# The ends of a SwiGLU FFN in a one-core decoder trunk: later operand sums and transposes, a spilled residual moved in the program, and one 16-k-tile block in place of a reduced one

## The chip, the core and the metric

The kernel runs on one core of a Trainium2 chip. The metric is the device time of one execution in microseconds (us); what is given below is the median of three runs, beside one profiled execution that the trace was taken from. TensorE (PE) multiplies, VectorE (DVE) and ScalarE (ACT) work on tiles, GpSimd (POOL) and SyncE (SP) issue DMAs, each in the order of its own instruction stream.

## What is computed

A trunk of two layers over 256 positions of width 2048, all in float32. Layer 0 mixes with SSD heads and latent attention, layer 1 with stick-breaking attention; each layer ends in a SwiGLU FFN with a hidden width of 5632, and this is what the change is about:

```
for layer in range(2):
    h = rms_norm(x, mix_norm[layer])
    x = x + mixer(h)
    x = x + swiglu_ffn(rms_norm(x, ffn_norm[layer]), w_gate[layer], w_up[layer], w_down[layer])
return rms_norm(x, final_norm)

def swiglu_ffn(h, w_gate, w_up, w_down):
    return (silu(h @ w_gate) * (h @ w_up)) @ w_down
```

## The kernel before

**Products.** A float32 operand is kept as two parts, hi and lo (hi is the value cast to a shorter float, lo the rest), and a product is three matmuls: hi by weight-hi, lo by weight-hi, hi by weight-lo. Weights come from memory as tiles of 128 x 2048 (1 MB), four k-tiles of 128 rows by 512 columns; ACT casts the hi part into one of the tiles named wh (L316, through wsplit), DVE subtracts to leave lo in place (L322). Both are in program order on their engines, and PE reads them after. The row of a tile that PE needs next is therefore always "cast on ACT, then split on DVE".

**Blocks.** An FFN has eleven blocks of 512 hidden columns. `gate_up(n)` calls `pair`, which computes both gate and up for a block over all 16 k-tiles by a Strassen-like scheme: seven products M1 to M7 over the first eight k-tiles, on sums of operand tiles and of weight tiles (wsub, L673: tiles named wsum), and the plain products c0 to c3 over the other eight. This order is `HALF`. The order `MORE` runs the scheme over 12 k-tiles: in place of c0 and c1 stand four half-size tiles n0 to n3, whose weight sums are t1 to t4. HALF has 180 matmuls of 512 columns a block (7 x 12 + 4 x 24), MORE 174 (84 + 2 x 24 + 42). MORE needs the operand sums N, made by `more_sums` on DVE and ACT from the third quarter of the normed input (xT[2]). Before the change blocks n = 0 and 1 are HALF, blocks 2 to 10 MORE.

**Order of the work.** PE runs in program order. A generator task sleeps a number of steps, and a step is a call of `tick`: two in a product of four k-tiles, one a k-tile in `project`, so about six matmuls. `more_sums` sleeps 1 step after it is spawned and `transpose_split` for h (the block's output, which becomes the operand of the down projection) 6. The other engines are ordered by a scheduler from priorities: weights by a counter, transposes of h and evacuations as urgent.

**h and the residual.** `right` ends a block's hidden tile with L852 on DVE and sends it through a DMA on POOL's queue to a tile of another type ("s<-s", L855); PE transposes what has landed (L327). The residual sits in the tile xres. It is written to memory as four quarters (saved) as each is ready, by POOL DMAs in norm_block (L465) and norm_operand (L536); from block 1 on, `lend` gives xres's space to the weight pools as two slots (tiles named lent0 and lent1), and each down projection adds its part into saved by an accumulating DMA (L871). After block 10, `load_residual` reads saved back into xres (L552), and the last three blocks' down projection (12 k-tiles, four `project` calls, L421 to L424) adds to xres. Blocks 0 and 1 have no down projection behind them; after each block from 2 on run two `project` calls of 8 k-tiles.

Of the kernel before, what the change touches and what calls it, by code (L numbers as in the profile page):

```python
# [15 lines left out]
P = 128  # L16
# [5 lines left out]
HID = 5632  # L22
# [18 lines left out]
class Trunk:  # L41
# [289 lines left out]
    def transpose_split(self, src, res, g=None, wait=3, rank=None):  # L331

        for k2 in range(2):
            yield wait if k2 == 0 else 1
            pt = self.tr([2, S])
            for k in range(2):
                for t in range(2):
                    self.transpose(pt[:, k, t * P:(t + 1) * P], src(t, 2 * k2 + k))
            hi, lo = self.s2([2, S], F32R), self.s2([2, S], F32R)
            if g is None:  # L340
                with self.urgent() if rank == self.URGENT else self.priority(rank or self.tc.cur_priority):
                    self.split(hi, lo, pt)
            else:
                with self.urgent() if rank == self.URGENT else self.priority(rank or self.tc.cur_priority):
                    gk = [g[:, kk:kk + 1] for kk in (2 * k2, 2 * k2 + 1)]
                    for k in range(2):
                        act = self.nc.scalar.activation(hi[:, k], pt[:, k], AF.Copy, scale=gk[k])
                    for k in range(2):
                        dve = self.nc.vector.scalar_tensor_tensor(lo[:, k], pt[:, k], gk[k], hi[:, k].bitcast(F32),
                                                                  op0=ALU.mult, op1=ALU.subtract)  # L350
                if rank and rank >= 99000 and k2 == 0:
                    self.first = [act.ins, dve.ins]
            res.append((hi, lo))
# [101 lines left out]
    def norm_block(self, st, j, g, wait=2, rank=None, blocks=False, spill=None, pause=2):  # L455

        x, res = self.xres, []

        def gen():
            yield from self.transpose_split(  # L460
                lambda t, k: x[:, t, j * 512 + k * P:j * 512 + (k + 1) * P], res, g[:, 4 * j:4 * j + 4], wait, rank)
            for t in range(2):
                self.square_sum(x[:, t, j * 512:(j + 1) * 512], st["ssq"][:, t, j:j + 1])
            if spill is not None:
                self.nc.gpsimd.dma_start(spill[j], x[:, :, j * 512:(j + 1) * 512])  # L465
        st["xT"].append((self.spawn(gen()), res))
        if blocks and j == 1:
            self.make_sums(st, pause)
# [36 lines left out]
    def more_sums(self, st):  # L505

        sub = lambda o, p, q: self.nc.vector.tensor_tensor(o, p, q, op=ALU.subtract)
        add = lambda o, p, q: self.nc.vector.tensor_tensor(o, p, q, op=ALU.add)
        yield 1
        self.join(st["xT"][2][0])  # L510
        a = {}
        for j, (hi, lo) in enumerate(st["xT"][2][1]):
            r = self.s2([2, S])
            add(r, hi.bitcast(F32), lo.bitcast(F32))
            a.update({(t, j): r[:, :, t * P:(t + 1) * P] for t in range(2)})
        yield 1
        s12, s34 = self.s2([4, P]), self.s2([4, P])
        s1, s2, s3, s4 = s12[:, :2], s12[:, 2:], s34[:, :2], s34[:, 2:]
        add(s1, a[1, 0], a[1, 1])
        sub(s2, s1, a[0, 0])  # L520
        sub(s3, a[0, 0], a[1, 0])
        sub(s4, a[0, 1], s2)
        for s in (s12, s34):
            yield 1
            hi, lo = self.s2([4, P], F32R), self.s2([4, P], F32R)
            self.split(hi, lo, s)
            st["N"].append((hi, lo))

    def norm_operand(self, st, j, g):

        x = self.xres

        def squares():
            for t in range(2):
                self.square_sum(x[:, t, j * 512:(j + 1) * 512], st["ssq"][:, t, j:j + 1])
            self.nc.gpsimd.dma_start(self.saved[j], x[:, :, j * 512:(j + 1) * 512])  # L536
        self.operand_block(st, j, lambda t, k: x[:, t, j * 512 + k * P:j * 512 + (k + 1) * P],
                           g[:, 4 * j:4 * j + 4], squares, 9)

# [125 lines left out]
        w.left = uses  # L665
        return wh, wl, w

    def wsub(self, o, p, q, so=None, sp=None, sq=None):

        half = lambda w, n: w.raw if n is None else w.raw[:, 2 * n:2 * n + 2]  # L670
        with self.priority(self.wprio):
            self.wprio += 100
            ins = self.nc.vector.tensor_tensor(half(o, so), half(p, sp), half(q, sq), op=ALU.subtract).ins  # L673
        for w in (p, q):
            w.readers.append(ins)
        if not o.readers:
            self.filled(o, ins)
# [8 lines left out]

    LATE = ("M1", "M5", "M3", "M6", "M2", "M7", "M4", "c0", "c1", "c2", "c3")

    def pair(self, st, va, vb, left, right, order=HALF):

# [85 lines left out]
        for m in order:  # L778
            if m == "t1":
                src["n2"] = self.wsum()  # L780
                self.wsub(src["n2"], raw["c1"], raw["c0"], 0, 0, 0)
                continue
            if m == "t2":
                self.wsub(src["n2"], raw["c1"], src["n2"], 1, 1, 0)
                continue
            if m == "t3":
                self.wsub(raw["c1"], raw["c1"], raw["c1"], 0, 1, 0)
                continue
            if m == "t4":
                src["n3"] = self.wsum()  # L790
                self.wsub(src["n3"], raw["c0"], src["n2"], 0, 1, 1)
                continue
            if m == "n0":
                halves(self.wsplit(raw["c0"], 4, 4, mybir.DependencyClass.Sync), ("M1", True), ("M2", False))
                continue
            if m == "n2":
                halves(self.wsplit(src["n2"], 4, 4, mybir.DependencyClass.Sync), ("M5", True), ("M6", False))
                continue
            if m == "n1":
                halves(self.wsplit(raw["c1"], 4), ("M7", False), ("M3", False))  # L800
                continue
            if m == "n3":
                halves(self.wsplit(src["n3"], 2, 2), ("M4", False))
                continue
            if m == "M1":
                self.wsub(t1, b12, b11)
                if more:
                    load("c0", "c1")
            if m == "M5":
                self.wsub(t2, b22, t1)  # L810
            if m == "M3":
                self.wsub(b12, b22, b12)
            if m == "M6":
                load("b21")
                b21 = src["M2"] = raw["b21"]
                src["M4"] = self.wsum()
                self.wsub(src["M4"], b21, t2)
            if m[0] == "c":
                load(m)
                src[m] = raw[m]  # L820
            w = self.wsplit(src[m], 8 if m[0] == "c" else 4)
            if m[0] == "c":
                k0 = 8 + int(m[1]) // 2 * 4
                x = [[self.operand_tile(st, k0 + k, t) for k in range(4)] for t in range(2)]
                for b in ("z", "p3") if int(m[1]) % 2 else ("p2", "p4"):
                    add(b, x[b in ("z", "p4")], w)
                continue
            add(bank[m], ops(m), w, m if m in keeps else None)

    def lend(self):  # L830

# [4 lines left out]
    def ffn(self, layer, st, gain_next):  # L836
# [3 lines left out]
        h = [None, None]  # L840
# [16 lines left out]

        def gate_up(n):
            self.pair(st, self.cols(wg, n * 512), self.cols(wu, n * 512), left, right,
                      self.MORE if n >= 2 else self.HALF)  # L860
            res = []
            return self.spawn(self.transpose_split(
                lambda t, k, h=tuple(h): h[t][:, k * P:(k + 1) * P], res, wait=6, rank=self.URGENT)), res

        def down(act, n0, n):
            ps = self.project(self.pairs(act), self.cols(wd, n * 512, r0=n0 * 512), 4 * len(act))
# [4 lines left out]
                nc.gpsimd.dma_start(self.saved[n][:, t], s, accum_op=ALU.add)  # L871

        act, held = [], []
        for n in range(HID // 512):
            if n == 1:
                self.lend()
            act.append(gate_up(n))
            for c in held[:2]:
                down(*c)
            held = held[2:]  # L880
            if len(act) == 2 and n < 8:
                held = [(act, n - 1, c) for c in range(4)]
                act = []
        nst = self.norm_begin()
        self.slots["w"] = self.slots["w"][:self.LOW]
        self.slots["wsum"] = self.slots["wsum"][:self.SUMS]
        self.load_residual(lambda j: self.saved[j])
        for n in range(4):
            if gain_next is None:
                self.final(n, self.pairs(act), self.cols(wd, n * 512, r0=8 * 512), 12)  # L890
# [77 lines left out]
    def norm_next(self, st, n, g):  # L968
        if n < 2:
            self.norm_operand(st, n, g)  # L970
        else:
            self.norm_block(st, n, g, 2 if n == 2 else 6, self.URGENT, spill=self.saved)
            if n == 2:
                st["more"] = self.spawn(self.more_sums(st))

# [520 lines left out]
```

## Time and profile before

| | |
|---|---|
| median of three runs | 2420.68 us (2420.16 to 2421.95) |
| the profiled execution | 2423.95 us, its span 2422.2 us |
| mean granted TensorE clock | 0.996 |
| PE, DVE, ACT, POOL busy, share of the span | 98%, 83%, 60%, 10% |
| FFN of layer 0, first block's first product to last block's last | about 632 us to 1265 us into the span |
| FFN of layer 1, the same | about 1711 us to 2345 us |

The profile's rows name line, engine, operation and tile (out<-in, buffer numbers left out), the count, and the idle time of the engine ahead of them with what ended it. A row of the timeline begins with the start in us from the span's start and the length. PE's matmuls overlap in the rows (a 128x512 matmul lasts some 0.39 us in a row and the next one starts 0.23 us after it), so distances are read from start to start.

### The profile page before, as it was taken

The numbers are of one execution on the slowest core, as the hardware profiler recorded it, in microseconds if no ns is written. First come the engines' busy times: TensorE is split into PE (matmuls) and PEld (weight loads), VectorE is DVE, ScalarE is ACT, GpSimd is POOL, SyncE is SP. The second block draws the span as 40 slices with busy tenths as digits, with TensorE's granted clock in tenths as the row PEclk, the third lists the DMA queues.
The fourth block names the chain that finished last, engine by engine and source line by source line (L and its number), as shares of the span: only waits on it lengthen the run. The fifth ranks groups of instructions, "written<-read, shape, count | busy, mean of one in ns | idle before, by whom it ended". The sixth has DMA issues, their size and how long they took to land.

```text
span 2422.2 us, 28061 instructions
## 1 busy us (share of the span) xinstructions
PE 2382.6 (98%) x10936; PEld 1956.7 (81%) x10936; DVE 2007.2 (83%) x1664; ACT 1463.6 (60%) x1480; POOL 233.8 (10%) x301
## 2 busy tenths in 40 slices
PE   8999999999999999999999999999999999999998
PEld 7888888777778888888888888888778888888877
DVE  6776597578999888888887989779998888998874
ACT  6665465555755665656655686775655565666663
POOL 1342001120000000000010010000000000000011
PEclk9999999999999999999999999999999999999999
DMA  7655556434656777777776555556667777777773
GB/s 261 201 182 192 186 191 186 117 131 156 222 196 226 221 232 230 220 233 235 224 222 225 199 175 180 184 174 226 211 206 229 224 226 224 227 226 229 226 251 119
DMA packets 274902, 497.88 MB, mean 206 GB/s; under 512 B 22924, under 2 KB 48144, under 8 KB 274768
## 3 DMA queue, kind: packets, MB, share of 16 engines
q1 hardware_dynamic: 255440, 446.48, 55.7%
q0 software_dynamic: 18752, 48.55, 8.0%
q8 instruction: 86, 1.41, 0.2%
q10 hardware_dynamic: 576, 1.05, 0.1%
q14 instruction: 48, 0.39, 0.0%
HBM read 459.24 MB, written 25.20 MB: 200 GB/s over the span
## 4 chain that ended last, share of the span: by engine, by line
PE 73%; issue 13%; DVE 9%; DMA 2%; POOL 2%; ACT 1%; SPq 0%; POOLq 0%; DVEq 0%; ACTq 0%
PE acc L726 39%; PE acc L421 10%; PE acc L424 10%; PE acc L423 10%; DVE wsum L673 2%; DVE wsum L322 2%; DVE w L322 2%; DMA s<-s 1%; DVE lent L322 1%; DVE lent L673 1%; PE at L1341 1%; PE tr L327 1%; DVE w L673 0%; POOL s L1245 0%; DVE s L322 0%
## 5 line engine op out<-in xcount | busy, mean ns | idle before, releaser
L322 DVE TENSOR_TENSOR w<-w,wh 128x2048 fp32r<-128x2048 f32 (+2 forms) x397 | 885.8, 2242 | 199.4 <-ACT wh L316 189.4
L726 PE MATMUL acc<-wh,s 128*128 128x512 f32 x3888 | 991.6, 393 | 7.3 <-DVE s L322 3.1
L316 ACT CAST wh<-w 128x2048 fp32r<-128x2048 f32 (+2 forms) x397 | 741.6, 1874 | 350.1 <-PE acc L424 133.8
L726 PEld LDWEIGHTS acc<-wh,s 128*128 128x128 f32 x3888 | 727.4, 189 | 160.1 <-ACT s L747 4.3
L421 PE MATMUL acc<-wh,s 128*128 128x512 f32 (+1 forms) x1280 | 510.8, 399 | 2.0 <-ACT wh L316 2.0
L424 PE MATMUL acc<-wh,s 128*128 128x512 f32 (+1 forms) x1280 | 496.9, 388 | 0.0
L423 PE MATMUL acc<-w,s 128*128 128x512 f32 (+1 forms) x1200 | 464.9, 387 | 0.0
L726 PE MATMUL acc<-w,s 128*128 128x512 f32 x1304 | 355.7, 391 | 0.4 <-DVE w L322 0.4
L726 PEld LDWEIGHTS acc<-w,s 128*128 128x128 f32 x1304 | 245.7, 189 | 53.5 <-DVE w L322 1.8
L424 PEld LDWEIGHTS acc<-wh,s 128*128 128x128 f32 x1280 | 240.8, 188 | 50.3
L421 PEld LDWEIGHTS acc<-wh,s 128*128 128x128 f32 x1280 | 241.2, 188 | 48.0 <-ACT wh L316 2.4
L423 PEld LDWEIGHTS acc<-w,s 128*128 128x128 f32 x1200 | 226.3, 189 | 43.6 <-issue 1.4
L316 ACT CAST wh<-wsum 128x2048 fp32r<-128x2048 f32 x103 | 186.7, 1813 | 74.7 <-DVE wsum L673 53.3
L322 DVE TENSOR_TENSOR wsum<-wsum,wh 128x2048 fp32r<-128x2048 f32 x103 | 222.8, 2163 | 4.0 <-ACT wh L316 4.0
L316 ACT CAST wh<-lent 128x2048 fp32r<-128x2048 f32 (+1 forms) x66 | 120.5, 1836 | 75.4 <-DMA lent<-in_w_gate_dram 33.6
L322 DVE TENSOR_TENSOR lent<-lent,wh 128x2048 fp32r<-128x2048 f32 (+1 forms) x66 | 144.0, 2186 | 8.6 <-ACT wh L316 8.2
L673 DVE TENSOR_TENSOR wsum<-w,wsum 128x2048 f32<-128x2048 f32 (+1 forms) x52 | 106.1, 2041 | 25.0 <-PE acc L726 20.9
L726 PE MATMUL acc<-wsum,s 128*128 128x512 f32 x388 | 109.2, 396 | 5.9 <-DVE wsum L322 5.3
L747 ACT COPY s<-acc 128x512 f32<-128x512 f32 x132 | 77.0, 584 | 57.2 <-PE acc L726 57.0
L855 POOL DMA_DIRECT2D s<-s x44 | 24.5, 557 | 783.7 <-DVE s L852 733.9
L726 PEld LDWEIGHTS acc<-wsum,s 128*128 128x128 f32 x388 | 72.1, 189 | 26.3 <-DVE wsum L322 11.8
L871 POOL DMA_DIRECT2D saved<-s x64 | 56.5, 1026 | 331.1 <-ACT s L870 331.1
(262 smaller groups left out, 1868.6 us busy)
## 6 DMA issues: line engine op xcount, KB each, us to landing
w<-in_w_down_dram SPq DMA_DIRECT2D x78, 1024.0 KB, 5.0
w<-in_w_gate_dram SPq DMA_DIRECT2D x76, 1024.0 KB, 5.1
w<-in_w_up_dram SPq DMA_DIRECT2D x76, 1024.0 KB, 5.2
w<-in_w_qkv_dram SPq DMA_DIRECT2D x48, 1024.0 KB, 5.0
w<-in_w_in_dram SPq DMA_DIRECT2D x47, 1024.0 KB, 5.1
w<-in_w_out_even_dram SPq DMA_DIRECT2D x32, 1024.0 KB, 5.0
saved<-s POOLq DMA_DIRECT2D x64, 256.0 KB, 6.7
w<-in_w_out_odd_dram SPq DMA_DIRECT2D x16, 1024.0 KB, 4.9
```

What stands on the lines that cost most here:

```text
L316: cast = nc.scalar.copy(hi, src).ins
L322: return nc.vector.tensor_tensor(lo, src, hi.bitcast(F32), op=ALU.subtract).ins
L327: self.nc.tensor.transpose(out.bitcast(F32R), src, self.ident_r)
L421: nc.tensor.matmul(ps[t], hi[:, ts], wh, start=k == 0, stop=False)
L423: slot.used(nc.tensor.matmul(ps[t], hi[:, ts], wl, start=False, stop=False), self.clock)
L424: nc.tensor.matmul(ps[t], lo[:, ts], wh, start=False, stop=k == nk - 1)
L673: ins = self.nc.vector.tensor_tensor(half(o, so), half(p, sp), half(q, sq), op=ALU.subtract).ins
L726: m = nc.tensor.matmul(ps[b], x, y, start=b not in started, stop=stop, skip_group_check=True)
L747: self.kept = nc.scalar.copy(o, ps[b]).ins
L855: nc.gpsimd.dma_start(words.bitcast(F32), h[t])
L871: nc.gpsimd.dma_start(self.saved[n][:, t], s, accum_op=ALU.add)
L1341: nc.tensor.matmul(py[:, ds], rows[c, h // 4][:, h % 4], xdt[c][:, ds], start=True, stop=True)
```

## The change

Five edits. `more_sums` sleeps 40 steps instead of 1. The transposes of h sleep 10 steps instead of 6, but for the last block's, which stay at 6. MORE begins at block 3 instead of block 2. The writing of the residual is taken out of the norm blocks and made a task of the FFN (`residual_away`, four DMAs 4 steps apart, joined ahead of `lend`); reading it back is a task too (`residual_back`, 12 steps, then 6 each). And block 0's subtraction for M3 is told to stand behind the last operand split of the third quarter (`lo`) in the order of DVE.

```
     def more_sums(self, st):
...
-        yield 1
+        yield 40
         self.join(st["xT"][2][0])
...
     def norm_operand(self, st, j, g):
...
-            self.nc.gpsimd.dma_start(self.saved[j], x[:, :, j * 512:(j + 1) * 512])
...
-    def wsub(self, o, p, q, so=None, sp=None, sq=None):
+    def wsub(self, o, p, q, so=None, sp=None, sq=None, after=None):
...
-        with self.priority(self.wprio):
+        with self.priority(self.wprio), self.tc.issue_after(after) if after else nullcontext():
...
             if m == "M3":
-                self.wsub(b12, b22, b12)
+                self.wsub(b12, b22, b12, after=st["lo"] if after == "lo" else after)
...
+    def residual_back(self):
+        for j in range(4):
+            yield 12 if j == 0 else 6
+            self.nc.gpsimd.dma_start(self.xres[:, :, j * 512:(j + 1) * 512], self.saved[j])
+
+    def residual_away(self):
+        for j in range(4):
+            yield 4
+            self.nc.gpsimd.dma_start(self.saved[j], self.xres[:, :, j * 512:(j + 1) * 512])
...
-                      self.MORE if n >= 2 else self.HALF)
+                      self.MORE if n >= 3 else self.HALF, None if n else "lo")
...
-                lambda t, k, h=tuple(h): h[t][:, k * P:(k + 1) * P], res, wait=6, rank=self.URGENT)), res
+                lambda t, k, h=tuple(h): h[t][:, k * P:(k + 1) * P], res, wait=10 if n < HID // 512 - 1 else 6, rank=self.URGENT)), res
...
+        away = self.spawn(self.residual_away())
         for n in range(HID // 512):
             if n == 1:
+                self.join(away)
                 self.lend()
...
-        self.load_residual(lambda j: self.saved[j])
+        self.spawn(self.residual_back())
...
-            self.norm_block(st, n, g, 2 if n == 2 else 6, self.URGENT, spill=self.saved)
+            self.norm_block(st, n, g, 2 if n == 2 else 6, self.URGENT)
```

How this moves instructions, at three places. **VectorE, block 0 of layer 0's FFN, ahead of M6's split.** In the rows, w_77, w_79 and wsum_83 are the splits of c0, M3 and M6 (written as the low part), wsum_82 and w_76 are weight sums, s are operand tiles; the rows with s alone are the operand sums N and their splits. Before:

```order
L508 TENSOR_TENSOR s_650_4940<-s_643_4918,s_644_4919 128x512
L508 TENSOR_TENSOR s_651_4942<-s_646_4929,s_647_4930 128x512
L322 TENSOR_TENSOR w_77<-w_78,wh_67 128x2048
L508 TENSOR_TENSOR s_652_4952<-s_650_4940,s_651_4942 128x256
L507 TENSOR_TENSOR s_653_4953<-s_650_4940 128x256
L507 TENSOR_TENSOR s_652_4952<-s_652_4952,s_650_4940 128x256
L673 TENSOR_TENSOR w_76<-w_80,w_76 128x2048
L507 TENSOR_TENSOR s_653_4953<-s_651_4942,s_652_4952 128x256
L322 TENSOR_TENSOR s_656_4968<-s_652_4952,s_655_4967 128x512
L322 TENSOR_TENSOR w_79<-w_80,wh_68 128x2048
L322 TENSOR_TENSOR s_658_4980<-s_653_4953,s_657_4979 128x512
L673 TENSOR_TENSOR wsum_82<-w_70,wsum_84 128x2048
```

After (the lines are numbered two or so higher):

```order
L322 TENSOR_TENSOR w_77<-w_78,wh_67 128x2048
L560 TENSOR_TENSOR xres<-s_622_4732,xres 128x512
L349 SCALAR_TENSOR_TENSOR s_644_4925<-tr_4919,va,s_643_4924 128x256 x2
L349 SCALAR_TENSOR_TENSOR s_648_4945<-tr_4939,va,s_647_4944 128x256 x2
L675 TENSOR_TENSOR w_76<-w_80,w_76 128x2048
L322 TENSOR_TENSOR w_79<-w_80,wh_68 128x2048
L349 SCALAR_TENSOR_TENSOR s_654_4986<-tr_4980,va,s_653_4985 128x256 x2
L675 TENSOR_TENSOR wsum_82<-w_70,wsum_84 128x2048
L349 SCALAR_TENSOR_TENSOR s_657_5001<-tr_4995,va,s_656_5000 128x256 x2
L322 TENSOR_TENSOR wsum_83<-wsum_84,wh_65 128x2048
```

The eight sums and splits have left this place, and both pairs of L349 of the last quarter now stand ahead of wsum_83, where before the second pair stood behind it. The eight rows are found again in block 1, between M3's split and M4's.

**TensorE, the end of block 10 in layer 0.** L726 (L728 after) is a product of pair; acc is its sum, lent_91 and lent_93 are low parts in xres's space. Before, the pair's last rows are

```order
L726 MATMUL acc_8555<-wh_67,s_664_5020 128x512
L726 MATMUL acc_8555<-wh_67,s_665_5021 128x512
L726 MATMUL acc_8555<-wh_67,s_664_5020 128x512
L726 MATMUL acc_8555<-wh_67,s_665_5021 128x512
L726 MATMUL acc_8555<-lent_93,s_661_5005 128x512 x2
L726 MATMUL acc_8555<-lent_93,s_664_5020 128x512 x2
```

and the last products with a lent tile after the change are

```order
L728 MATMUL acc_8552<-wh_67,s_631_4794 128x512
L728 MATMUL acc_8552<-wh_67,s_632_4795 128x512
L728 MATMUL acc_8552<-lent_91,s_631_4794 128x512 x4
L728 MATMUL acc_8554<-wh_68,s_625_4760 128x512
L728 MATMUL acc_8554<-wh_68,s_626_4761 128x512
```

Which slot a tile gets has shifted, since block 2 makes fewer sums: the pair's last products no longer read a lent tile, and 78 matmuls of the pair follow those that do. The same holds in layer 1.

**GpSimd, the DMAs around block 10's h in layer 0.** s_898 and s_899 are the two halves of h. Before:

```order
L871 DMA saved_89<-s_888_8545 128x512
L871 DMA saved_89<-s_889_8548 128x512
L552 DMA xres<-saved_86 128x2x512
L552 DMA xres<-saved_87 128x2x512
L552 DMA xres<-saved_88 128x2x512
L855 DMA s_898_8773<-s_897_8744 128x512
L855 DMA s_899_8789<-s_894_8628 128x512
L552 DMA xres<-saved_89 128x2x512
```

After:

```order
L883 DMA saved_89<-s_888_8543 128x512
L883 DMA saved_89<-s_889_8546 128x512
L835 DMA xres<-saved_86 128x2x512
L835 DMA xres<-saved_88 128x2x512
L835 DMA xres<-saved_87 128x2x512
L835 DMA xres<-saved_89 128x2x512
L867 DMA s_898_8771<-s_897_8742 128x512
L867 DMA s_899_8787<-s_894_8626 128x512
```

All four reads of the residual now stand ahead of both halves of h. The four writes of the residual stand in POOL's order where they stood.

More of the change, by code (lines that the diff above doesn't have):

```diff
@@ L350, in transpose_split @@
                                                                   op0=ALU.mult, op1=ALU.subtract)
+                self.lo = dve.ins
                 if rank and rank >= 99000 and k2 == 0:
@@ L461, in gen @@
                 lambda t, k: x[:, t, j * 512 + k * P:j * 512 + (k + 1) * P], res, g[:, 4 * j:4 * j + 4], wait, rank)
+            if j == 2:
+                st["lo"] = self.lo
             for t in range(2):
@@ L687, with pair @@
     LATE = ("M1", "M5", "M3", "M6", "M2", "M7", "M4", "c0", "c1", "c2", "c3")
-    def pair(self, st, va, vb, left, right, order=HALF):
+    def pair(self, st, va, vb, left, right, order=HALF, after=None):
         nc = self.nc
```

## The prediction

> **What bounds the kernel now.** I began with the busy shares and then took the table of what PE waited for.
>
> ```profile
> PE 2382.6 (98%) x10936; PEld 1956.7 (81%) x10936; DVE 2007.2 (83%) x1664; ACT 1463.6 (60%) x1480; POOL 233.8 (10%) x301
> PE tr L327 <- DMA s<-s: 8.5, 6, 2.0
> PE acc L726 <- DVE wsum L322: 5.3, 2, 2.6
> ```
>
> PE is busy 98% of the span, so it is the bound, and only its waits and its number of matmuls can move the time. The columns of the waits are the sum in us, how often, and the longest. The two largest in the FFNs are the transposes of h, which wait for the DMA that changes h's type, and M6's product, which waits for its split. They are what the five edits touch, so I went to those places in the timeline. First block 0 of layer 0:
>
> ```profile
> 647.77 1.97 PE L726 MATMUL acc<-wh,s 128*128 128x512 f32 x8
> 652.38 1.20 PE L726 MATMUL acc<-wsum,s 128*128 128x512 f32 x4 [2.63 <-DVE wsum L322]
> 653.41 3.51 PE L726 MATMUL acc<-wh,s 128*128 128x512 f32 x8
> ```
> ```profile
> 686.79 1.07 PE L726 MATMUL acc<-w,s 128*128 128x512 f32 x4
> 689.59 0.51 PE L327 MATMUL tr<-ident_r,s 128*128 128x128 f32 x4 [1.73 <-DMA s<-s]
> ...
> 731.86 1.07 PE L726 MATMUL acc<-lent,s 128*128 128x512 f32 x4
> 733.49 0.51 PE L327 MATMUL tr<-ident_r,s 128*128 128x128 f32 x4 [0.56 <-DMA s<-s]
> ...
> 1273.14 0.39 PE L424 MATMUL acc<-wh,s 128*128 128x512 f32 x1
> 1275.18 0.50 PE L327 MATMUL tr<-ident_r,s 128*128 128x128 f32 x4 [1.66 <-DMA s<-s]
> ```
>
> Eight matmuls last 1.97 us and a single one 0.39, so one starts (1.97 - 0.39) / 7 = 0.2265 us after another. From start to start, less what the matmuls between need: M6 lost 652.38 - 647.77 - 8 x 0.2265 = 2.80 us; the transposes behind block 0 lost 1.89, those behind block 1 0.72, those behind block 10 1.81. Each is about 0.16 more than the idle time in brackets.
>
> Layer 1 has the same four places. Its waits from block 0 to the transposes behind block 1, and the row behind its block 10:
>
> ```profile
> PE tr L327 <- DMA s<-s: 2.9, 2, 2.0
> PE acc L726 <- DVE wsum L322: 2.6, 1, 2.6
> PE acc L726 <- DVE w L322: 0.2, 1, 0.2
> 2355.28 0.50 PE L327 MATMUL tr<-ident_r,s 128*128 128x128 f32 x4 [1.68 <-DMA s<-s]
> ```
>
> With 0.16 more for each, that is 2.80 for M6, 3.2 for the two pairs of transposes, 1.84 at the end. Together the two layers lose 5.6 at M6, 2.61 + 3.2 = 5.8 at the transposes behind blocks 0 and 1, and 3.65 behind block 10: **15.0 us**, and 0.2 at c0 in layer 1.
>
> Each wait can cost twice. The eight matmuls after M6's wait last 3.51 us instead of 1.97. Busy times in 3.4 us behind three of the waits (the figure ahead of DMA share and GB/s is the granted clock):
>
> ```profile
> 653.50:656.90 3.40, 3.40 (x10) 2.65 (x9) 3.40 (x3) 3.15 (x6) 0.00 (x0) 0.50 0.38 67
> 1275.00:1278.40 3.40, 3.22 (x19) 2.76 (x20) 1.13 (x3) 1.17 (x2) 0.00 (x0) 1.00 0.92 357
> 1769.70:1773.10 3.40, 3.40 (x14) 2.71 (x13) 0.83 (x2) 1.17 (x2) 0.00 (x0) 0.50 0.02 5
> ```
>
> Behind M6 and behind block 0's transposes, in both layers, the clock is 0.50 for 3.4 us (the first and the last of four such stretches are shown); behind block 10 it stays 1.00. Half speed over 3.4 us is 1.7 us lost: 4 x 1.7 = **6.8 us** hang on waits of 1.73 to 2.63 us. That the gate goes with the wait is what I take from it.
>
> [...]
>
> **Part a: operand sums 40 steps later.** DVE in block 0, from ahead of c0's split to M6's:
>
> ```profile
> 636.70 1.28 DVE L508 TENSOR_TENSOR s<-s,s 128x512 f32<-128x512 f32 x2
> 637.90 2.28 DVE L322 TENSOR_TENSOR w<-w,wh 128x2048 fp32r<-128x2048 f32 x1
> 640.10 0.42 DVE L508 TENSOR_TENSOR s<-s,s 128x256 f32<-128x256 f32 x1
> ...
> 641.11 2.28 DVE L673 TENSOR_TENSOR w<-w,w 128x2048 f32<-128x2048 f32 x1
> 643.31 0.41 DVE L507 TENSOR_TENSOR s<-s,s 128x256 f32<-128x256 f32 x1
> ...
> 644.25 2.28 DVE L322 TENSOR_TENSOR w<-w,wh 128x2048 fp32r<-128x2048 f32 x1
> 646.45 0.68 DVE L322 TENSOR_TENSOR s<-s,s 128x512 fp32r<-128x512 f32 x1
> 647.05 2.28 DVE L673 TENSOR_TENSOR wsum<-w,wsum 128x2048 f32<-128x2048 f32 x1
> 649.25 0.87 DVE L349 SCALAR_TENSOR_TENSOR s<-tr,va,s 128x256 fp32r<-128x256 f32 x2
> 650.04 2.28 DVE L322 TENSOR_TENSOR wsum<-wsum,wh 128x2048 fp32r<-128x2048 f32 x1
> ```
>
> DVE has no gap here. The sums and their splits take 637.90 - 636.70 = 1.20, 641.11 - 640.10 = 1.01, 644.25 - 643.31 = 0.94 and 647.05 - 646.45 = 0.60: 3.75 us that leave. By the order, the second pair of L349 comes ahead of M6's split (0.79, as the first pair: 650.04 - 649.25). So the split comes 2.97 us earlier, and PE, which read its result at 652.38, could at 649.41. PE itself is there at 647.77 + 8 x 0.2265 = 649.58: the wait goes, with 0.17 us to spare. That is thin, but a miss of 0.3 costs 0.3 and hardly the clock, which stayed at 1.00 behind 1.66 us. Telling block 0's subtraction for M3 to stand behind `lo` changes only this order and is in the count. Value: -2.80 a layer and -1.7 for the clock.
>
> The eight instructions come back in block 1, between M3's split and M4's. There DVE has room:
>
> ```profile
> 668.93 0.69 DVE L846 TENSOR_TENSOR s<-acc,s 128x512 f32<-128x512 f32 x1 [1.67 <-PE acc L726]
> 681.88 1.40 DVE L852 SCALAR_TENSOR_TENSOR s<-s,rstd,s 128x512 f32<-128x512 f32 x2
> ...
> 697.15 2.29 DVE L322 TENSOR_TENSOR lent<-lent,wh 128x2048 fp32r<-128x2048 f32 x1
> 704.66 1.07 PE L726 MATMUL acc<-lent,s 128*128 128x512 f32 x4
> ```
>
> M4's split (the lent tile) was done at 699.4, and PE came to it at 704.66, 5.2 us later. After the change PE comes 8.1 us earlier (2.80 + 1.7 + 1.89 + 1.7), at 696.6. DVE starts the stretch behind L852 5.4 us earlier (next part) and must do 3.75 us more in it and one weight sum of 2.2 us that the order shows moved behind L852; it saves the gaps in which it stood waiting for h's transposes, and those now come later. Adding the rows of the order from 677.8 on, each by its length here, gives M4's split ready at about 696.1 and M7's at 698.9 against 699.3: estimates with half a microsecond to spare. I take nothing for it; the upper bound is a rival.
>
> **Part b: transposes of h 10 steps.** By the order the transposes behind a block stand 24 matmuls later, 5.44 us. The low clock and the wait ahead of them gone, PE reaches block 0's old place 4.5 us earlier (2.80 + 1.7). h's last step on DVE was 681.88; DVE ahead of it waited 1.67 us for PE (668.93) and that goes with PE's own shift, so both halves are issued some 5.4 us earlier, at about 678. What a transfer takes is the view of the issues at L855, of block 10 of layer 0 and then of all blocks from 690 to 1250 us:
>
> ```profile
> DMA to landing us min/median/max: 5.9/5.9/5.9
> ...
> DMA to landing us min/median/max: 2.3/2.6/5.9
> ```
>
> By the longest, 5.9, block 0's h has landed at 684, and PE comes at 689.59 - 1.89 - 4.5 + 5.44 = 688.6: 4.6 us to spare. Behind block 1 h was 0.72 late and now has 5.44 more, less what PE gains over DVE. Those waits go: -5.8, and -3.4 for the two slow stretches behind block 0. In the other blocks PE did not wait here, and h's splits, 1.2 us of DVE, only come later; the down projection that reads them starts two blocks later.
>
> **Part c: the residual.** The four writes keep their place in POOL's order and their releasers: nothing. The reads matter behind block 10:
>
> ```profile
> 1265.67 2.18 POOL L552 DMA_DIRECT2D xres<-saved  x3 [33.62 <-PE acc L726]
> 1268.51 1.22 POOL L855 DMA_DIRECT2D s<-s  x2 [0.65 <-DVE s L852]
> ```
>
> Three reads of 512 KB went out at 1265.7 to 1267.8, held until PE's last use of a lent tile, and h's halves behind them took 5.9 us instead of the median 2.6: they landed late. The order shows that all four reads now stand ahead of h, but the last products with a lent tile are 78 matmuls earlier: they are issued 78 x 0.2265 = 17.7 us earlier, and long done when h goes out at 1268.5. With 2.6 us h lands at about 1271.8, ahead of 1273.37, where PE is due. The step of 6 for the last block is kept. Value: -1.81 and -1.84. The lower bound is nothing: the transfer stays at 5.9.
>
> **Part d: block 2 as HALF.** 180 matmuls instead of 174 in each layer: 12 x 0.2265 = **+2.7 us**. The six fewer half tiles also spare DVE work there. In the trace, DVE's later blocks have no PE wait on DVE, so nothing else comes of it but time for the sums.
>
> **The sum.** -15.0 - 6.8 - 0.2 + 2.7 = **-19.3 us**. The profiled execution took 2423.95, so its like would take 2404.7; the median of the runs is 2420.68, 3.3 below it, and I take the same 19.3 from that: **2401.4 us**. If a few tenths stay at M6 and M4, they count for some 0.5 each.
>
> **Rivals.**
> - DVE late in block 1. The half microsecond to spare at M4 and M7 is an estimate, and the sums may come late enough for a wait there of up to 2.0 us, plus 1.7 for the clock: 3.7 a layer, 7.4 in all, **2408.8**. For it: DVE ran 16 us in block 0 without a gap. Against it: 5.2 us to spare at 704.66.
> - The end stays. The reads are still in flight when h goes out, or weights slow h just as well (the DMA share is 0.92 behind 1275): +3.65, **2405.1**.
> - The clock gates anyway, wherever PE's time stands: +6.8, **2408.2**. Against it: four of four waits of 1.7 and more in blocks 0 and 1 show it, and nothing beside them.
> - The change only moves the deficit: what is taken out of block 0 is missing as much in block 1, so parts a and b come to nothing, with their clock: +18.2, **2419.6**, no change.
> - Slower: DVE becomes the bound from M6 of block 0 through block 1, and its deficit is taken in four waits instead of two. If DVE is about 1.8 us late at each of M6, the transposes, M4 and M7, every one with a slow stretch, a layer loses 4 x (1.8 + 1.7) = 14.0 there in place of some 9.2. With the end's gain and block 2's cost: 2420.7 + 2 x 4.8 - 3.65 + 2.7 = **2429.4**. It decides from about 1.7 us late at each, where rows of this trace show the clock fall; my estimates would all be wrong by 2 us or more.
>
> **How the numbers follow.** Forecast 0.66, 2399 to 2404; DVE late 0.14; the end stays 0.07; the clock gates anyway 0.03; only moved 0.05; slower 0.05. The range of 8 in 10 takes in the first four, of which the third and second reach 2408.8, with the small leftovers on top: 2398.5 to 2410.5; below, 2.9 us for a slow stretch and some tenths that I have not seen. A change of 0.2%, 4.8 us, is about what a measurement of this kernel can tell from none. Only the last two rivals are not faster by that: faster 0.90, same 0.05, slower 0.05.
>
> **What would show it.** In the profile after: no wait on wsum L322 in block 0 over 0.5 us; no wait on "s<-s" behind blocks 0, 1 and 10; a clock of 1.00 in both FFNs; h of block 10 landing in about 2.6 us; 10948 PE instructions for 10936. A wait of M4 or M7 on L322 in block 1 with a clock of 0.50 behind it proves me wrong on DVE; 0.50 without a wait ahead of it, on the clock.

## The result, and the profile after

The changed kernel takes **2401.8 us** (six runs, 2401.46 to 2402.44) beside 2420.99 for the kernel before (six runs, 2418.32 to 2421.95): a ratio of 0.9921, interval 0.9909 to 0.9934. The forecast was 2401.4. The profiled execution took 2401.46, its span 2399.7. One execution of the kernel before among the later runs took 2959.38 us at a granted clock of 0.753; it is left out of every ratio below. The page's busy shares, PE from 580 to 2390 us (both FFNs and what lies between them; the figure ahead of DMA share and GB/s is the granted clock), then PE at M6 and at the transposes behind blocks 0 and 1 of layer 0:

```profile
PE 2375.5 (99%) x10948; PEld 1955.1 (81%) x10948; DVE 1992.2 (83%) x1652; ACT 1460.5 (61%) x1476; POOL 233.8 (10%) x301
```
```profile
580.00:2390.00 1810.00, 1805.57 (x8169) 1490.68 (x8167) 1576.19 (x1089) 1122.77 (x1019) 125.75 (x158) 1.00 0.68 216
```
```profile
645.17 1.98 PE L728 MATMUL acc<-wh,s 128*128 128x512 f32 x8
647.01 1.20 PE L728 MATMUL acc<-wsum,s 128*128 128x512 f32 x4
...
685.23 1.07 PE L728 MATMUL acc<-w,s 128*128 128x512 f32 x4
686.14 0.46 PE L327 MATMUL tr<-ident_r,s 128*128 128x128 f32 x4
...
726.83 1.07 PE L728 MATMUL acc<-w,s 128*128 128x512 f32 x4
727.74 0.46 PE L327 MATMUL tr<-ident_r,s 128*128 128x128 f32 x4
```

There are 12 more matmuls, as counted, the clock is at 1.00 in both FFNs, and none of the three places has a wait: from 645.17 to 647.01 are 1.84 us for eight matmuls that need 1.81, from 685.23 to 686.14 and from 726.83 to 727.74 0.91 each, which is four matmuls. Of PE's waits in the two FFNs one row is left, at M6 in layer 1:

```profile
PE acc L728 <- DVE wsum L322: 0.2, 1, 0.2
```

DVE ahead of M6, its split for M4 in block 1, and PE's first product that reads this split:

```profile
643.89 0.87 DVE L349 SCALAR_TENSOR_TENSOR s<-tr,va,s 128x256 fp32r<-128x256 f32 x2
644.67 2.28 DVE L322 TENSOR_TENSOR wsum<-wsum,wh 128x2048 fp32r<-128x2048 f32 x1
...
691.09 2.28 DVE L322 TENSOR_TENSOR lent<-lent,wh 128x2048 fp32r<-128x2048 f32 x1
```
```profile
694.19 1.07 PE L728 MATMUL acc<-lent,s 128*128 128x512 f32 x4
```

M6's split ends at 646.95 and PE starts at 647.01: the 0.17 us to spare that were worked out were in truth none, and the wait went all the same. M4's split ended at 693.4, 0.8 us before PE came to it; the working had 696.1 in the old kernel's time, where PE started the eight matmuls ahead of M6's wait 2.6 us later (647.77 against 645.17), so 693.5, with half a microsecond to spare. GpSimd around block 10 of layer 0, and the time from issue to landing of h there:

```profile
1237.35 2.89 POOL L835 DMA_DIRECT2D xres<-saved  x4 [16.40 <-PE acc L728]
1257.90 1.21 POOL L867 DMA_DIRECT2D s<-s  x2 [17.66 <-DVE s L864]
```
```profile
DMA to landing us min/median/max: 2.5/2.5/2.6
```

The four reads went out 20 us ahead of h, and h landed in 2.5 us instead of 5.9. In layer 1 only the half that is issued last gained. Its rows, and the time to landing there:

```profile
2306.75 2.92 POOL L835 DMA_DIRECT2D xres<-saved  x4 [17.81 <-PE acc L728]
2324.70 0.57 POOL L867 DMA_DIRECT2D s<-s  x1 [15.02 <-DVE s L864]
2328.16 0.55 POOL L867 DMA_DIRECT2D s<-s  x1 [2.89 <-DVE s L864]
```
```profile
DMA to landing us min/median/max: 2.9/4.3/5.7
```

The first half took 5.7 us, more than the 4.2 of the kernel before, though the last read had landed at 2317.0, 7.7 us before it was issued; so reads ahead of h are not the only thing that slows it. The second half took 2.9 us instead of 5.7 and landed at 2331.1, in time for the transposes at 2332.19.

### The profile page after: what moved, and what is told of

It is laid out like the page before. It is cut to its first block, busy times and chain, and to the rows that moved or that the text cites. A ratio compares the mean times of both kernels' runs of the same rounds, so it can differ in the third digit from the quotient of the medians.

```text
span 2399.7 us, 28017 instructions
## 1 busy us (share of the span) xinstructions
PE 2375.5 (99%) x10948; PEld 1955.1 (81%) x10948; DVE 1992.2 (83%) x1652; ACT 1460.5 (61%) x1476; POOL 233.8 (10%) x301
## 4 chain that ended last, share of the span: by engine, by line
PE 88%; issue 5%; DVE 5%; DMA 1%; ACT 1%; POOL 0%; ACTq 0%; SPq 0%; POOLq 0%; DVEq 0%
PE acc L728 48%; PE acc L422 11%; PE acc L425 11%; PE acc L424 11%; DVE wsum L675 1%; DVE wsum L322 1%; PE at L1432 1%; PE at L1355 1%; DVE lent L675 1%; DVE w L322 1%; DVE lent L322 1%; PE tr L327 1%; PE tr L363 1%; PE at L1431 0%; PE tr L329 0%
## 5 line engine op out<-in xcount | busy, mean ns | idle before, releaser
L728 PE MATMUL acc<-wh,s 128*128 128x512 f32 x3896 | 987.2, 391 | 7.4 <-DVE s L322 3.3
L728 PEld LDWEIGHTS acc<-wh,s 128*128 128x128 f32 x3896 | 726.1, 188 | 157.8 <-DVE s L322 4.2
L424 PE MATMUL acc<-w,s 128*128 128x512 f32 (+1 forms) x1216 | 471.1, 387 | 0.0
L728 PE MATMUL acc<-w,s 128*128 128x512 f32 x1312 | 356.7, 390 | 0.2 <-DVE w L322 0.2
L728 PEld LDWEIGHTS acc<-w,s 128*128 128x128 f32 x1312 | 246.8, 188 | 52.3 <-DVE w L322 0.6
L316 ACT CAST wh<-wsum 128x2048 fp32r<-128x2048 f32 (+1 forms) x101 | 182.8, 1809 | 80.5 <-DVE wsum L675 47.4
L322 DVE TENSOR_TENSOR wsum<-wsum,wh 128x2048 fp32r<-128x2048 f32 (+1 forms) x101 | 218.5, 2163 | 6.2 <-ACT wh L316 6.2
L316 ACT CAST wh<-lent 128x2048 fp32r<-128x2048 f32 (+1 forms) x62 | 114.5, 1857 | 82.1 <-DVE lent L675 28.9
L322 DVE TENSOR_TENSOR lent<-lent,wh 128x2048 fp32r<-128x2048 f32 (+1 forms) x62 | 137.0, 2217 | 8.3 <-ACT wh L316 8.1
L728 PE MATMUL acc<-wsum,s 128*128 128x512 f32 x380 | 105.9, 393 | 0.8 <-DVE wsum L322 0.2
L728 PEld LDWEIGHTS acc<-wsum,s 128*128 128x128 f32 x380 | 70.4, 188 | 20.0 <-DVE wsum L322 5.7
```

Source lines behind the costliest of these rows:

```text
L316: cast = nc.scalar.copy(hi, src).ins
L322: return nc.vector.tensor_tensor(lo, src, hi.bitcast(F32), op=ALU.subtract).ins
L424: slot.used(nc.tensor.matmul(ps[t], hi[:, ts], wl, start=False, stop=False), self.clock)
L728: m = nc.tensor.matmul(ps[b], x, y, start=b not in started, stop=stop, skip_group_check=True)
```

## Experiments

Medians, and ratios to the kernel before, run together with it on the same chip each time. The runs e1 to e4, e5 to e8 and e9 to e12 were made on three different chips. "From the change" is the distance from 2401.8 and so goes across chips: taken from the ratios instead it differs by up to 2.5 us, and by the intervals a distance of less than about 3 us is not told from none. The waits are those of PE in the two FFNs, start to start; M6's 0.4 us in layer 1 is left out where others stand.

| run | us | ratio to before (interval) | from the change | waits in the FFNs of its profile |
|---|---|---|---|---|
| e1 sums at 1 step | 2410.04 | 0.9952 (0.9940 to 0.9965) | +8.2 | M6 2.78, 2.79 |
| e2 transposes at 6 steps | 2411.93 | 0.9965 (0.9951 to 0.9978) | +10.1 | transposes 2.18, 2.47, 1.71, 2.37 |
| e3 reads without a task | 2400.56 | 0.9915 (0.9901 to 0.9928) | -1.2 | M6 0.41 in layer 1 |
| e4 M3 not behind lo | 2403.17 | 0.9927 (0.9915 to 0.9940) | +1.4 | c0 1.22, 1.59 |
| e5 12 k-tiles from the third block | 2409.35 | 0.9944 (0.9929 to 0.9959) | +7.6 | block 10 2.06, 3.24; third block 1.24, 1.28 |
| e6 the same, h ahead of the reads | 2401.43 | 0.9909 (0.9893 to 0.9925) | -0.4 | third block 1.25, 1.25 |
| e7 transposes at 7 steps | 2406.51 | 0.9931 (0.9916 to 0.9946) | +4.7 | transposes 1.36, 1.27, 0.67, 1.36 |
| e8 before again | 2419.15 | one run | | as before |
| e9 as e6, first h at 48 steps | 2401.52 | 0.9917 (0.9903 to 0.9932) | -0.3 | third block 0.90, 0.90 |
| e10 sums alone | 2415.60 | 0.9972 (0.9961 to 0.9983) | | see below |
| e11 writes in the norm blocks | 2401.75 | 0.9915 (0.9900 to 0.9930) | -0.1 | M6 0.44 in layer 1 |
| e12 transposes alone | 2412.19 | 0.9960 (0.9946 to 0.9973) | | see below |

### One edit undone: the sums

```
-        yield 40
+        yield 1
```

> The changed kernel (2401.8 us) with the operand sums back at 1 step after the spawn; the other four edits stay. As the prediction's part a prices it: M6's split is late again by 2.8 us in each layer, with 1.7 us at half clock behind it, 9.0 us in all: 2410.8. If the low clock isn't tied to the wait: 5.6 us, 2407.4. If the sums were hidden anyway: 2401.8.

Measured 2410.04. The profile has M6's waits, whole:

```profile
PE acc L728 <- DVE wsum L322: 5.3, 2, 2.6
```

5.6 us of waits, and the clock at 0.50 for 3.4 us behind both (mean granted clock 0.997, beside 0.998 in the profile of the change): part a holds, and in this execution its price for the clock too. The time is near the first of the three figures; whether the clock always falls with these waits is not yet told apart.

### One edit undone: the transposes of h

```
-  ... wait=10 if n < HID // 512 - 1 else 6, rank=self.URGENT ...
+  ... wait=6, rank=self.URGENT ...
```

> The changed kernel with the transposes of h at 6 steps in every block. If the terms of the prediction add up, part b is undone: +5.8 and +3.4 for two slow stretches, 2411.0. Rival, from the trace of the changed kernel: h lands there 3.5, 3.2, 3.2 and 3.1 us ahead of the transposes behind blocks 0 and 1 of the two layers, and 24 matmuls are 5.44 us; so all four waits come out at 1.9 to 2.4 us, 8.8 in all, each with a slow stretch of 1.7 behind it, also behind block 1 where the kernel before had none: +15.6, 2417.4. If part a alone had brought h in time: 2401.8.

The waits are those of the rival, 8.7 us in all; the time, 2411.93, lies far below its 2417.4. PE's waits in layer 0 up to the transposes behind block 1, the same in layer 1, and PE in 3.4 us behind the first and the second of them:

```profile
PE tr L327 <- DMA s<-s: 4.3, 2, 2.3
...
PE tr L327 <- DMA s<-s: 3.8, 2, 2.2
```
```profile
683.20:686.60 3.40, 3.40 (x21) 2.84 (x21) 1.80 (x3) 1.85 (x3) 0.00 (x0) 1.00 0.02 5
726.80:730.20 3.40, 3.07 (x13) 2.61 (x14) 0.69 (x1) 0.60 (x2) 0.00 (x0) 0.50 0.00 0
```

Two waits of nearly one length, 2.18 and 2.47, and the granted clock is 1.00 behind the one and 0.50 behind the other; behind the two of layer 1 it is 1.00 as well. 8.7 and one slow stretch of 1.7 are 10.4, beside the 10.1 measured. So a low clock does not follow from a wait of such length. The other reading: with the rest of the change in place, the 4 steps are worth more than in the old kernel (8.7 of waits against 5.8). The second halves of h, for which PE waits, took 6.3 to 6.6 us to land in this trace and 5.4 to 5.8 in that of the kernel before; the four differences add up to 3.1 us. What makes them longer is not shown.

### The reads as one piece, and the writes in the norm blocks

```
-        self.spawn(self.residual_back())
+        self.load_residual(lambda j: self.saved[j])
```

> The changed kernel, but the four reads of the residual are written in one piece at the end of the blocks, as before the change, and not as a task of 12 and then 6 steps. If the earlier last use of a lent tile is what frees h's DMA (the prediction's part c), they are still issued some 18 us ahead of h: 2401.8, no wait behind block 10. If the spacing of the task frees it: +3.65, 2405.4, with waits of 1.7 us on h's DMA behind block 10 in both layers.

```profile
1234.94 2.90 POOL L554 DMA_DIRECT2D xres<-saved  x4 [15.73 <-PE acc L728]
1255.49 1.21 POOL L867 DMA_DIRECT2D s<-s  x2 [17.66 <-DVE s L864]
```

The reads stand where they stood, and no wait is behind block 10: the task isn't what frees h. This profile also lacks one slow stretch in the mixer, worth 1.7 us, that the profile of the changed kernel has (at 576.0 us, last section; the mean granted clock is 0.999 here and 0.998 there); the median's 1.2 us below the change fit that, and are no gain of this edit. e11 put the writes back into the norm blocks (spill given to `norm_block`, one DMA in `squares`, no `residual_away`):

> The changed kernel with the residual written by the norm blocks, as before the change, and only its reading a task. The prediction costs the writes at nothing, since they keep their place in GpSimd's order: 2401.8 within 0.5 and the clock's raster. If the norm blocks' writes had held something up: some us more, with a wait in block 0.

2401.75, and no wait in block 0. The residual's two tasks are worth nothing here.

### M3's subtraction not held behind lo

```
-                      self.MORE if n >= 3 else self.HALF, None if n else "lo")
+                      self.MORE if n >= 3 else self.HALF)
```

> The changed kernel without the order that puts block 0's subtraction for M3 behind the third quarter's last split. By the prediction, which gave this edit no price of its own, 2401.8. Rival: the second pair of L349 of the third quarter then stands behind that subtraction, is done at about 638.7 us of the changed kernel's trace, and c0 reads it at 637.2: a wait of 1.5 us in each layer, which takes away 0.2 at M6 in layer 1: +2.8, 2404.6, or +6.2 with a slow stretch behind each.

DVE and PE at c0:

```profile
634.16 2.28 DVE L675 TENSOR_TENSOR w<-w,w 128x2048 f32<-128x2048 f32 x1
636.36 0.87 DVE L349 SCALAR_TENSOR_TENSOR s<-tr,va,s 128x256 fp32r<-128x256 f32 x2
```
```profile
636.89 0.96 PE L728 MATMUL acc<-wh,s 128*128 128x512 f32 x3 [1.06 <-DVE s L349]
```

The rival holds: c0 waits for a split that the subtraction has pushed back. The edit that the prediction gave no price repairs what the later sums would otherwise break: 2.8 us of waits less 0.4 that M6 then saves, 2.4. The median moved by 1.4 only, which the scatter does not tell from nothing, and this profile too lacks the slow stretch in the mixer (mean granted clock 0.999); it is the waits that show what the edit does.

### 12 k-tiles from the third block

```
-                      self.MORE if n >= 3 else self.HALF, None if n else "lo")
+                      self.MORE if n >= 2 else self.HALF, None if n else "lo")
```

> The changed kernel with the 12-k-tile blocks from the third block on again; the sums at 40 steps, the tasks of the residual and the rest stay. 12 matmuls fewer: -2.7 us. If the tiles' rotation is what brought the last use of a lent tile forward (the prediction's part c), the reads stand ahead of h's DMA again and both waits behind block 10 come back, 1.81 and 1.84: in all +0.95, 2402.8. If the task that reads the residual back is what freed h: 2399.1.

GpSimd at block 10, then two rows of PE's waits over the whole program:

```profile
1256.73 2.18 POOL L835 DMA_DIRECT2D xres<-saved  x3 [36.03 <-PE acc L728]
1259.53 1.22 POOL L867 DMA_DIRECT2D s<-s  x2 [0.62 <-DVE s L864]
```
```profile
PE tr L327 <- DMA s<-s: 5.0, 2, 3.1
...
PE acc L728 <- DVE w L322: 1.6, 3, 0.7
```

Three reads stand ahead of h again, though the task is there, and they go out behind the last product with a lent tile, which starts at 1255.36 us here and at 1235.85 in the changed kernel. With e3 this shows that the lent tiles' rotation, and so the third block as HALF, is what brought part c's gain. But 2409.35 is far above 2402.8. The waits behind block 10 came out at 2.06 and 3.24, with slow stretches behind both in the profiled run (in layer 0, 512-column matmuls of 0.63 us in the rows from 1267.40 to 1270.13; mean granted clock 0.997, beside 0.998), and the third block itself waits 2.5 us, most of it for DVE. e6 keeps the 12 k-tiles from the third block and takes the reads out of h's way:

```
-            nc.gpsimd.dma_start(words.bitcast(F32), h[t])
+            self.words = nc.gpsimd.dma_start(words.bitcast(F32), h[t]).ins
...
-            self.nc.gpsimd.dma_start(self.xres[:, :, j * 512:(j + 1) * 512], self.saved[j])
+            with self.tc.issue_after(self.words):
+                self.nc.gpsimd.dma_start(self.xres[:, :, j * 512:(j + 1) * 512], self.saved[j])
```

> As the run before it, but the four reads of the residual are ordered behind the DMAs of the last block's h on GpSimd's queue. If h is late only for the reads ahead of it, no wait behind block 10 and 12 matmuls fewer than in the changed kernel: 2399.1. If the reads then come too late for the adds to the residual that end the first of the last four column blocks: waits of several us on them, above 2402.

```profile
1258.80 1.20 POOL L868 DMA_DIRECT2D s<-s  x2 [37.12 <-DVE s L865]
1260.32 2.84 POOL L836 DMA_DIRECT2D xres<-saved  x4 [0.32 <-issue]
```
```profile
727.15 0.73 PE L728 MATMUL acc<-w,s 128*128 128x512 f32 x2 [0.67 <-DVE w L322]
...
733.02 2.14 PE L728 MATMUL acc<-wh,s 128*128 128x512 f32 x8 [0.24 <-ACT s L749]
```

No wait behind block 10, and the adds to the residual are in time. Yet 2401.43 is no better than the change: the 2.7 us that 12 matmuls cost are spent again in the third block, 1.25 in each layer; in layer 0 DVE has had two gaps from 655 us up to the first wait there, of 0.36 and 0.15 us. e9 takes the splits of the first block's h out of DVE's way:

```
-  ... wait=10 if n < HID // 512 - 1 else 6, rank=self.URGENT ...
+  ... wait=48 if n == 0 else 10 if n < HID // 512 - 1 else 6, rank=self.URGENT ...
```

> As the run with the 12-k-tile blocks from the third block and h's DMAs ahead of the reads (2401.43 us), but the transposes of the first block's h at 48 steps, behind the place in the third block where PE waited for DVE. The two splits of h, 1.2 us of DVE with a wait of 0.4 ahead of one, leave DVE ahead of that place. If DVE's work up to there sets the wait, its 0.83 us in each layer goes: 2399.8. If the weights or ACT set it: 2401.4. The raster of the clock can move either by 1.7.

```profile
714.50 0.69 DVE L864 TENSOR_TENSOR s<-acc,s 128x512 f32<-128x512 f32 x1 [0.64 <-PE acc L728]
```

The wait fell from 0.83 to 0.49 only, for two reasons. Of the 1.6 us of DVE set free, 0.4 are lost, most of it in this gap, where DVE waits for PE: counted from the product ahead of the place where h's transposes stood (685.63 us in e6, 686.19 here), the split that PE waits for ends 1.14 us earlier. And PE comes to it 0.77 us earlier as well, since the transposes that moved no longer stand ahead of it. 2401.52 does not differ from the change. No version here beats it by more than the runs scatter.

### Fewer steps, for the slack

```
-  ... wait=10 if n < HID // 512 - 1 else 6, rank=self.URGENT ...
+  ... wait=7 if n < HID // 512 - 1 else 6, rank=self.URGENT ...
```

> The changed kernel with the transposes of h at 7 steps instead of 10: 18 matmuls or 4.08 us earlier. With the 3.5, 3.2, 3.2 and 3.1 us to spare in its trace: waits of 0.6, 0.9, 0.9 and 1.0, in all +3.4, 2405.2, with the clock at 1.00 throughout. If the low clock follows any wait, 1.7 more for each: 2412. If h's time to land follows the place of the transposes: 2401.8.

4.7 us of waits, the mean granted clock at 0.998 as in the profile of the change, and 2406.51: +4.7. The waits exceed the expectation by 0.3 in the mean; one lies below it (0.67 for 0.9), one far above (1.36 for 0.6), so h's issue and landing vary by tenths from trace to trace.

### Single edits on the kernel before

```
-        yield 1
+        yield 40
```

> The kernel before with the operand sums at 40 steps as the only edit. By the prediction's terms, -5.6 for M6 and -3.4 for its clock: 2411.7 against 2420.7. If PE then only comes earlier to the transposes of h, as in the run with these at 6 steps (waits of 2.2, 2.5, 1.7 and 2.4 us, 8.8 in all, where the kernel before had 5.8 to 6.1), 2.7 to 3.0 of it are given back: 2414.5, and 2 or 3 us around it for the clock's raster; the waits behind block 10 stay, 1.8 each.

```profile
PE tr L327 <- DMA s<-s: 6.8, 6, 2.1
...
PE acc L726 <- DVE s L349: 2.5, 2, 1.4
PE acc L726 <- DVE w L322: 1.8, 3, 0.8
```

2415.6, and M6's waits are gone; about as much comes back as was expected, but not in the same places. The transposes behind blocks 0 and 1 waited 3.9 us, less than the 5.8 of the kernel before, where 8.8 were expected. What came instead is c0's wait (the one of e4: 1.22 and 1.61) and 0.96 and 0.95 for a weight split in the third block (as in e5 and e6).

```
-  ... res, wait=6, rank=self.URGENT ...
+  ... res, wait=10 if n < HID // 512 - 1 else 6, rank=self.URGENT ...
```

> The kernel before with the transposes of h at 10 steps (6 in the last block) as the only edit. The waits behind blocks 0 and 1 go, 5.8 to 6.1 us, and the slow stretches behind them, of which two traces of the kernel before show two each; M6's waits of 2.8 and those behind block 10 of 1.8 stay: 2420.7 - 5.9 - 3.4 = 2411.4. If the parts only work together: no gain, 2420.

```profile
PE acc L726 <- DVE wsum L322: 5.3, 2, 2.6
...
PE tr L327 <- DMA s<-s: 2.6, 2, 1.9
```

2412.19, 10.1 us below the kernel before in the same group of runs (2422.3), where e10 lies 6.7 below: this edit alone gives the larger part. It leaves M6 as it was (5.6), and block 10 of layer 0 waits 2.0 us, of layer 1 0.8.

### The kernel before again

> The kernel before once more, for a second sample of its clock. If the low clock belongs to a wait of about 1.7 us or more (the prediction), the same four slow stretches in the FFNs: behind M6 and behind block 0's transposes in both layers. If it hangs on how a wait lies against a fixed raster of 3.4 us, as the runs at 1 and at 6 steps suggest (two of two waits of 2.8, one of four of 1.7 to 2.5), some of them are gone or stand elsewhere while the waits are the same.

M6's wait in layer 0, then PE in 3.4 us behind it and behind block 0's transposes:

```profile
651.13 1.20 PE L726 MATMUL acc<-wsum,s 128*128 128x512 f32 x4 [2.63 <-DVE wsum L322]
652.16 1.99 PE L726 MATMUL acc<-wh,s 128*128 128x512 f32 x8
```
```profile
652.00:655.40 3.40, 3.40 (x16) 2.48 (x14) 3.40 (x3) 3.40 (x7) 0.00 (x0) 1.00 0.25 34
...
687.40:690.80 3.40, 3.40 (x14) 2.81 (x14) 0.70 (x2) 1.17 (x2) 0.00 (x0) 0.51 0.02 5
```

The idle time is 2.63 us to the hundredth, as in the first trace, and here the clock stays at 1.00: eight matmuls take 1.99 us, not 3.51. Two slow stretches instead of four, and 2419.15 instead of 2423.95.

## Why the prediction was right, and where it was not

**M6.** Right in place and size: e1 brings back 5.6 us of waits by this one number.

**Transposes of h.** Right in the mechanism; all four waits went. The slack was 3.5 us (686.14 less the landing at 682.6), not 4.6, since h took 6.5 us to land, where 5.9 was taken as the longest. The term was sized by the old kernel's waits; undone within the change it is 8.7 (e2).

**Block 10.** The reads' earlier release frees h, as worked out, and the task has no part in it (e3, e5). In layer 1 it freed only the second half of h; the first took 5.7 us, so the rival's "weights slow h just as well" or something else like it is not ruled out there, but did not cost a wait. Where the prediction booked the third block as a cost of 2.7 us with nothing else to come of it, that edit carries this gain and spares the third block 2.5 us of waits as well: "In the trace, DVE's later blocks have no PE wait on DVE, so nothing else comes of it" was the failing step: it holds for the old kernel, but with the sums 40 steps later PE waits for DVE in a third block of 12 k-tiles (e5, e6, e10). Undoing the edit costs 7.6 us (e5).

**M3 behind lo.** Counted at nothing beside the order; it takes away 2.8 us of waits that the later sums would make (e4, e10).

**The clock.** This step failed. "That the gate goes with the wait is what I take from it" was read off one execution: the same wait of 2.63 us has the low clock in one trace and not in the other (e8). The 6.8 us were true of the profiled run, not of the median of all, from which they were subtracted. Between the second trace of before and that of the change, the spans fall by 2417.4 - 2399.7 = 17.7 us: waits of 14.9 in the FFNs (2.79, 2.11, 1.14, 1.83 and 2.79, 2.16, 0.66, 1.40) less 0.4 left at M6, 3.4 for two slow stretches, less 2.7 for the 12 matmuls, together 15.2, and 2.5 elsewhere. Of these, 1.4 lie ahead of M6's wait in layer 0, where none of the waits that the edits take away stands (PE started the eight matmuls ahead of it at 646.5 there and at 645.17 here); what makes these 1.4 is not shown, and the rest is spread and not explained. Between the first trace and the change it is 22.5. So the size of the gain depends on the execution it is measured against; that the forecast came within 0.4 us is partly luck, since the kernel before scatters from 2417.5 to 2426.5 us in fifteen runs taken together. What stands is the waits, 14.9 us gone but for 0.4, and 2.7 paid. The other 7 us of the 19.2 between the medians are slow stretches (two in one trace of the kernel before, four in the other, 3.4 and 6.8 us) and what differs elsewhere; no run splits them.

The rivals: DVE was not late at M4 or M7, nor were the reads still in flight when h went out; nothing moved the deficit elsewhere. The reading that the clock gates wherever PE's time stands had been given 0.03: it is as wrong as mine, since the low stretches in the FFNs are gone with the waits, but not each wait had one.

## What to carry to other kernels

Price a wait by its start-to-start distance, but price what the clock adds to it over several executions, never from one. Undo edits one at a time in the finished kernel: the parts here add to 27 us undone singly (8.2, 10.1, 1.4, 7.6) for a gain of 19. Undoing one can uncover waits that the kernel before did not have: 2.9 us more at the transposes in e2, 2.8 at c0 in e4, 2.5 in the third block in e5. A table that decides which buffer a tile gets can be worth more than the instructions that it adds or saves.

## What the runs showed of the hardware

**The low stretches of the clock, in these traces, lie on a raster of 3.413 us.** By the clock records of before, each of its five low stretches, apart from the one at the program's end, is 3.413 us long, and they begin at 578.4, 653.5, 691.1, 1732.1 and 1769.7 us, which lie 22.0, 11.0, 305.0 and 11.0 times 3.413 us apart; in the second trace, at 578.2, 687.4 and 1766.1, close to 32 and 316 times. Where the raster lies against the start of the span differs from execution to execution: the first record of the full clock begins at 15.2 us in the trace of before and at 12.8 in that of the change, and the first low stretch comes 563.2 us after it in both, which is 165.0 times 3.413.

PE's idle time was added up in each 3.413 us of this raster (distances between starts less 0.227 us for a 512-column matmul, gaps above 0.15 us), from the first record of the full clock to PE's last matmul. In the trace of before, the five low stretches come right behind 2.48, 2.26, 1.89, 2.79 and 2.13 us idle; of the other sums at the full clock the largest are 1.84 and 1.46. In that of the change the one low stretch ahead of the program's end, at 576.0 us, comes behind 2.46 us (layer 0's mixer has a wait of 2.5 us there), and of the other sums at the full clock the largest are 1.46 and 0.92. M6's 2.8 us in layer 0 lay in the first trace with 2.26 us in the 3.413 us ahead of the low stretch, and were split into 1.56 and 1.23 by the raster in the second, where the clock stayed at 1.00. No run varied the idle time alone.

**The landing of h varies.** The same transfer took 2.2 to 7.1 us in the changed kernel, 6.2 to 7.1 for seven of the eight halves behind blocks 0 and 1 and 3.7 for the eighth, 2.5 and 2.6 behind block 10 of layer 0, and 5.7 and 2.9 behind that of layer 1. The DMA engines' busy share alone does not order them: it was 0.91 from 675.6 to 682.6 us, where the halves took 6.5 and 6.6, 0.91 from 1257.9 to 1261.2, where they took 2.5 and 2.6, and 0.81 from 2324.7 to 2330.4, where one took 5.7. What sets the time no run here isolates.
